# Gate sums of an mLSTM layer: transposes in place of products with the identity, and a running sum by two products over partial sums

## The chip, the cores and the metric

The kernel runs on one core of a Trainium2 chip. The metric is the device time of the whole kernel in microseconds (us), as the median of several runs. The core has five engines that run side by side, each through a queue of its own in the order in which the program was compiled: TensorE (PE in the profile, with its weight loads as PEld), VectorE (DVE), ScalarE (ACT), GpSimd (POOL) and SyncE (SP, which only issues transfers here). Between engines they wait for each other by semaphores.

## The reference, cut to what matters

One decoder layer on 512 positions of 1024 channels. A normed input is projected to the columns of two groups: an mLSTM group of 4 heads of 256 channels, and a convolution group. Both outputs are joined, projected back, normed and added, and a convolutional feed-forward block follows. The change touches the gates of the mLSTM group and one norm of the convolution group. For each head there are two gates per position, an input gate and a forget gate:

```
lfc = jax.nn.log_sigmoid(chunks(f_pre))
...
b = jnp.cumsum(lf_, axis=-1)
dmat = jnp.where(causal, b[..., :, None] - b[..., None, :] + i_[..., None, :], -jnp.inf)
m_t = jnp.maximum(b + m[..., None], jnp.max(dmat, axis=-1))
...
h = num / jnp.maximum(jnp.abs(den), jnp.exp(-m_t))[..., None]
```

The kernel does not carry a state from chunk to chunk. With F the running sum of the log forget gates over all 512 positions and a = i - F, the weight of position s for position t is exp(a[s] - M[t]), where M is the running maximum of a; and exp(-(F + M)) bounds the denominator from below. The convolution group's outcome is normed over its channels, with one factor per position.

## The kernel before, in words

Positions stand as 4 blocks of 128 (NT = 4, P = 128), channels as 8 blocks of 128 (KT = 8). Large products are split into a high and a low part (hi, lo) and done as three products (mm3, L188 to L190). The stages are: reading and norming x; the projections of the convolution group (glu); values and gates of head 0 (make_v, L416); queries, keys and output gates of the heads (head_proj, L481); attention per head (L500); joining (mixa, mixb); the feed-forward block (up); and its last product and the output.

Gates: make_v(0) leaves the eight gate values of each position in gz, 128 partitions by 4 blocks by 8 values. L571 to L581 turn the forget gates into their log sigmoid lf (128 x 4 blocks x 4 heads) with small operations on ScalarE and VectorE. L615 to L618 then make the running sum F over 512 positions by TensorE: the triangle tri gives the sum inside a block, and products with ones, shifted by one, two and three blocks, add the blocks before. VectorE copies it out (Fc, L620) and forms ga = i - F (L621). L624 to L626 turn ga, so that heads stand on 4 partitions and positions along the row (aT). A scan on VectorE makes the running maximum Mr (L628), which is split into Ms (L630, L631) for the weights of each head (make_E, L598). L633 to L636 turn Mr back to positions on partitions (mtok), and L638 to L640 make em of it, the bound of the denominator.

Norm of the convolution group: the helper bcast (L199 to L204) spreads a factor per position over all partitions. It takes a column of 128 factors, lets it stand for 128 columns (to_broadcast), and multiplies it with the identity. It is called once, by rms_bcast (L206) in norm_rows (L772), with the name ry_b.

Order of the work: the queues of SP and TensorE follow the order in which the program is written (manual_schedule, L1333). The order on VectorE, ScalarE and GpSimd is made by a planner, from priorities and from times in its own plan; only the stages inside in_order() (the opening, the stretch between joining and feed-forward, and the output) are fixed by hand. The convolution taps (cv, L731, 25 per block of channels on VectorE, in cv_block at L714) have a lowered priority and fill VectorE's queue between other operations. On TensorE the order about the change is: three projections of head 0 (L611, L612), the running sum (L618), the fourth projection (L622), the turning of ga (L626), the fifth projection (L632), the turning of Mr (L636), the sixth (L642), and then head 0's attention. hn (L549) is the outcome of a head's attention after its norm; it is turned at L555. E (L515) are the products of scores and weights. The identity (ident), ones and tri are float32. A transpose elsewhere in the kernel (L555, L653, L902) is written as PE.transpose with the identity.

Of the kernel before, what the change touches and what calls it, by code (L numbers as in the profile page):

```python
# [10 lines left out]
F32 = mybir.dt.float32  # L11
# [3 lines left out]
ALU = mybir.AluOpType  # L15
PSUM = bass.MemoryType.PSUM

P = 128
# [3 lines left out]
NT = T // P  # L22
H = 4
# [29 lines left out]
def decoder_layer(ctx, tc, w_glu0, x, xT, c, adaT, vecs, w_glu, w_qko, w_v0, w_v, w_out, w_up, w_down, out):  # L53
    nc = tc.nc
    V, S, G, PE = nc.vector, nc.scalar, nc.gpsimd, nc.tensor

    const = ctx.enter_context(tc.tile_pool(name="const", bufs=1))
# [26 lines left out]
    def slot(name, dt=F32):  # L84
        return slots.tile([P, T], dt, tag="t", name=name)

    def mmbank(name):
        return psum.tile([P, T], F32, tag="mm", bufs=4, name=name)

    def atbank(name):  # L90
        return psum.tile([P, T], F32, tag="at", bufs=2, name=name)
# [9 lines left out]
    ident = const.tile([P, P], F32, name="ident")  # L101
    make_identity(nc, ident)
    ones = const.tile([P, P], F32, name="ones")
    V.memset(ones, 1.0)
    tri = const.tile([P, P], F32, name="tri")
# [93 lines left out]
    def bcast(col, n, name, bank=atbank):  # L199

        ps = bank(name)
        for i in range(n // P):
            PE.matmul(ps[:, i * P : (i + 1) * P], col[:, i : i + 1].to_broadcast([P, P]), ident, start=True, stop=True)
        return ps  # L204

    def rms_bcast(ps, n, scale, name, bank=atbank):  # L206
        m = n // P
        t = small.tile([P, NT], F32, tag="rt", name=f"{name}_t")
        V.tensor_scalar(out=t[:, :m], in0=ps[:, :m], scalar1=scale, scalar2=EPS, op0=ALU.mult, op1=ALU.add)
        r = small.tile([P, NT], F32, tag="rr", name=f"{name}_r")  # L210
        G.tensor_tensor(out=r[:, :m], in0=t[:, :m], in1=mhalf[:, :m], op=ALU.pow)
        return bcast(r, n, f"{name}_b", bank)
# [186 lines left out]
    for i in range(G0 // 2, KT):  # L399
        glu_weights(i)  # L400
        for half in range(2):
            ps = mmbank(f"glu{i}_{half}")
# [164 lines left out]
    def g16(name):  # L567
        return const.tile([P, NT, H], F32, name=name)

    fpre = gz[:, :, H : 2 * H]  # L570
    fa, fe, fu, fl, fr, lf = (g16(f"g_{i}") for i in ("fa", "fe", "fu", "fl", "fr", "lf"))  # L571
# [7 lines left out]
    V.tensor_tensor(out=fr, in0=fr, in1=fa, op=ALU.mult)  # L579
    V.tensor_tensor(out=fl, in0=fl, in1=fr, op=ALU.subtract)  # L580
    V.scalar_tensor_tensor(out=lf, in0=fpre, scalar=0.0, in1=fl, op0=ALU.min, op1=ALU.subtract)  # L581
    OFF = [0, 512, 896, 1152]
    NS = [T - cc * P for cc in range(NT)]

# [29 lines left out]

    fps = atbank("fcum")  # L615
    fv = fps[:, : NT * H].rearrange("p (t h) -> p t h", t=NT)
    for d in range(NT):
        PE.matmul(fps[:, d * H : NT * H], ones if d else tri, lf[:, : NT - d, :].rearrange("p t h -> p (t h)"), start=d == 0, stop=d == NT - 1)  # L618
    Fc, ga = g16("Fc"), g16("ga")
    V.tensor_copy(Fc, fv)  # L620
    V.tensor_tensor(out=ga, in0=gz[:, :, :H], in1=Fc, op=ALU.subtract)  # L621
# [1 line left out]

    aps = atbank("aT")  # L624
    for tt in range(NT):
        PE.matmul(aps[:H, tt * P : (tt + 1) * P], ga[:, tt, :], ident, start=True, stop=True)  # L626
    Mr = slot("Mr")[:H, :]
    V.tensor_tensor_scan(out=Mr, data0=aps[:H, :], data1=zero[:H, :].to_broadcast([H, T]), initial=0.0, op0=ALU.max, op1=ALU.max)  # L628

# [3 lines left out]
    mps = atbank("mtok")  # L633
    mv = mps[:, : NT * H].rearrange("p (t h) -> p t h", t=NT)
    for tt in range(NT):
        PE.matmul(mv[:, tt, :], Mr[:, tt * P : (tt + 1) * P], ident[:H, :H], start=True, stop=True)  # L636
    em = g16("em")
    V.tensor_tensor(out=em, in0=Fc, in1=mv, op=ALU.add)  # L638
    S.activation(em, em, AF.Exp, scale=-1.0)
# [394 lines left out]
    for i in range(NF):  # L1034
        if i < NE:
            pa, pg = early[i]
        else:
# [11 lines left out]
            for half in range(2):  # L1049
                ps = mmbank(f"up{i}_{half}")  # L1050
# [141 lines left out]
    for m in range(NM):  # L1192
# [5 lines left out]
        if M2 - NT <= m < M2:  # L1198
            tt = m - M2 + NT
# [138 lines left out]
```

## Time and profile before

| | us |
|---|---|
| median of 3 runs | 772.34 |
| lowest and highest run | 771.94, 775.13 |
| the profiled execution, its span from first to last instruction | 771.4 |
| busy in it: TensorE | 758.4 |
| VectorE | 610.1 |
| ScalarE | 403.8 |
| GpSimd | 352.2 |

The profile is of one execution of its own; the page gives its span, which lies 0.94 us below the median of the timed runs. A page of the profile gives busy times, then the span in forty equal slices with a digit for the busy tenths of each engine, then the chain of work that ended last, followed back from the last instruction to what released each step. Answers of the trace give the same by line, by stage or in order of time. In a timeline a row is a start, a duration and an instruction, several alike merged into one row with their count.

### The profile page before, as it was taken

To read this page: it belongs to the slowest core of one execution; us is meant where nothing else is said; L and a number is where in the kernel's file an instruction comes from. 1 tells how busy PE (TensorE), PEld (TensorE's weight loads), DVE (VectorE), ACT (ScalarE), POOL (GpSimd) and SP (SyncE) were. 2 spreads that over 40 slices of the span, in tenths; PEclk is the share of its full clock that TensorE was granted. 3 is DMA by queue.
4 is the path that set the end of the run, shared out by engine and by line. 5 is a ranking of instruction groups with operands and counts; after the bars stand their busy time and mean duration, and the time that the engine had idled before them with its cause. 6 is when DMAs were issued, how large, how long until landed. Compare 5 with 4: busy or idle time off the path is not lost.

```text
span 771.4 us, 10631 instructions
## 1 busy us (share of the span) xinstructions
PE 758.4 (98%) x3709; PEld 637.5 (83%) x3709; DVE 610.1 (79%) x967; ACT 403.8 (52%) x761; POOL 352.2 (46%) x286
## 2 busy tenths in 40 slices
PE   7999999999999999999999999999999999999996
PEld 5788898778888888988888998888888888888885
DVE  6997999999999966756768798666556687799995
ACT  5447266776666447582253555444444444455762
POOL 2029578696798645443661456444444440000001
PEclk9999999999999999999999999999999999999998
DMA  8983214214022452434953753332233321777872
GB/s 320 377 301 132 90 55 164 82 40 151 30 84 107 153 179 105 164 110 164 366 199 126 253 197 130 130 130 88 110 117 129 130 89 62 255 271 241 298 260 109
DMA packets 36409, 125.33 MB, mean 162 GB/s; under 512 B 4194, under 2 KB 5634, under 8 KB 30468
## 3 DMA queue, kind: packets, MB, share of 16 engines
q1 hardware_dynamic: 24372, 96.17, 35.5%
q10 hardware_dynamic: 11984, 28.48, 10.6%
q8 instruction: 29, 0.48, 0.3%
q14 instruction: 24, 0.20, 0.1%
HBM read 113.22 MB, written 11.42 MB: 162 GB/s over the span
## 4 chain that ended last, share of the span: by engine, by line
PE 72%; DVE 21%; DMA 2%; ACT 2%; issue 2%; POOL 0%; ACTq 0%; DVEq 0%; POOLq 0%
PE up L189 10%; PE up L188 10%; DVE cv L731 10%; PE up L190 10%; PE p L1185 4%; PE glu L189 3%; PE glu L190 3%; PE glu L188 3%; PE p L189 3%; PE p L188 3%; PE p L190 3%; PE mixa L188 2%; PE mixa L190 2%; PE mixa L189 2%; PE mixb L189 2%; PE mixb L188 2%
## 5 line engine op out<-in xcount | busy, mean ns | idle before, releaser
L731 DVE SCALAR_TENSOR_TENSOR cv<-gt,cvw,cv 128x505 f32<-128x505 f32 (+24 forms) x200 | 137.3, 729 | 2.3 <-ACT cv L719 1.1
L685 POOL TENSOR_TENSOR ro2r<-ro2t,mhalf 128x1 f32<-128x1 f32 x1 | 0.5, 537 | 119.8 <-DVE ro2t L683 119.8
L727 POOL TENSOR_TENSOR cs<-cs,cs 128x510 f32<-128x510 f32 (+3 forms) x32 | 41.9, 1308 | 0.3
L171 POOL TENSOR_TENSOR wup_1024l<-wup,wup_1024h 128x512 fp32r<-128x512 f32 x20 | 27.4, 1372 | 31.6 <-ACT wup_1024h L170 31.6
L171 POOL TENSOR_TENSOR wup_0l<-wup,wup_0h 128x512 fp32r<-128x512 f32 x20 | 27.7, 1387 | 30.0 <-ACT wup_0h L170 30.0
L171 POOL TENSOR_TENSOR wup_1536l<-wup,wup_1536h 128x512 fp32r<-128x512 f32 x20 | 28.0, 1399 | 27.6 <-ACT wup_1536h L170 25.1
L155 DVE SCALAR_TENSOR_TENSOR junk<-ada,cb 128x1024 bf16<-128x1024 f32 x20 | 31.3, 1565 | 8.5 <-DMA ada<-in_adaT 8.4
L189 PE MATMUL up<-u2l,wup_0h 128*128 128x512 f32 (+1 forms) x100 | 36.5, 365 | 0.2 <-DVE u2l L910 0.2
L188 PE MATMUL up<-u2h,wup_0h 128*128 128x512 f32 (+1 forms) x100 | 36.5, 365 | 0.0
L188 PE MATMUL up<-u2h,wup_1024h 128*128 128x512 f32 (+1 forms) x100 | 36.4, 364 | 0.0
L190 PE MATMUL up<-u2h,wup_0l 128*128 128x512 f32 (+1 forms) x100 | 36.4, 364 | 0.0
L188 PE MATMUL up<-u2h,wup_512h 128*128 128x512 f32 (+1 forms) x100 | 36.4, 364 | 0.0
L189 PE MATMUL up<-u2l,wup_512h 128*128 128x512 f32 (+1 forms) x100 | 36.4, 364 | 0.0
L190 PE MATMUL up<-u2h,wup_512l 128*128 128x512 f32 (+1 forms) x100 | 36.4, 364 | 0.0
L188 PE MATMUL up<-u2h,wup_1536h 128*128 128x512 f32 (+1 forms) x100 | 36.4, 364 | 0.0
L189 PE MATMUL up<-u2l,wup_1536h 128*128 128x512 f32 (+1 forms) x100 | 36.4, 364 | 0.0
L190 PE MATMUL up<-u2h,wup_1536l 128*128 128x512 f32 (+1 forms) x100 | 36.4, 364 | 0.0
L190 PE MATMUL up<-u2h,wup_1024l 128*128 128x512 f32 (+1 forms) x100 | 36.4, 364 | 0.0
L189 PE MATMUL up<-u2l,wup_1024h 128*128 128x512 f32 (+1 forms) x100 | 36.3, 363 | 0.0
L171 POOL TENSOR_TENSOR wup_512l<-wup,wup_512h 128x512 fp32r<-128x512 f32 x20 | 27.7, 1383 | 14.0 <-ACT wup_512h L170 14.0
L725 ACT ACTIVATE cs<-gt,cvw 128x511 f32<-128x511 f32 (+4 forms) x40 | 27.4, 716 | 6.5 <-POOL cs L727 3.2
L170 ACT ACTIVATE wup_1024h<-wup 128x512 fp32r<-128x512 f32 x22 | 13.9, 631 | 25.1 <-PE up L189 20.4
(1072 smaller groups left out, 2667.0 us busy)
## 6 DMA issues: line engine op xcount, KB each, us to landing
wup<-in_w_up SPq DMA_DIRECT2D x22, 1024.0 KB, 6.5
wqko<-in_w_qko SPq DMA_DIRECT2D x12, 1024.0 KB, 4.8
ada<-in_adaT ACTq DMA_DIRECT2D x20, 512.0 KB, 4.6
ada<-in_adaT SPq DMA_DIRECT2D x16, 512.0 KB, 6.9
wo<-in_w_out SPq DMA_DIRECT2D x8, 1024.0 KB, 4.8
spare<-in_adaT ACTq DMA_DIRECT2D x12, 512.0 KB, 7.4
wd<-in_w_down SPq DMA_DIRECT2D x6, 768.0 KB, 6.7
g2kept<-g2d SPq DMA_DIRECT2D x11, 384.0 KB, 7.3
```

Of the source, the lines that this page charges most:

```text
L155: t = V.scalar_tensor_tensor(out=junk, in0=r, scalar=1.0, in1=cb, op0=ALU.mult, op1=ALU.mult, accum_out=mod[:, i : i + 1])
L170: S.activation(hi[:, :n], src, AF.Copy)
L171: (eng or G).tensor_tensor(out=lo[:, :n], in0=src, in1=hi[:, :n].bitcast(F32), op=ALU.subtract)
L188: PE.matmul(ps, a[0], b[0], start=start, stop=False)
L189: PE.matmul(ps, a[0], b[1], start=False, stop=False)
L190: PE.matmul(ps, a[1], b[0], start=False, stop=stop)
L685: G.tensor_tensor(out=r, in0=t, in1=mhalf[:, :1], op=ALU.pow)
L725: S.activation(t[:, d:], cvx[j][:, : T - d], AF.Copy, scale=w(CK - 1 - d))
L727: G.tensor_tensor(out=side[:, d:], in0=side[:, d:], in1=t[:, d:], op=ALU.add)
L731: last_tap[0] = V.scalar_tensor_tensor(out=cp[:, d:], in0=cvx[j][:, : T - d], scalar=w(CK - 1 - d), in1=cp[:, d:], op0=ALU.mult, op1=ALU.add)
L1185: PE.matmul(ps[q], x, y, start=False, stop=m == NM - 1 and i == 2, skip_group_check=True)
```

## The change: what it does

Five edits. In bcast, at L626 and at L636 the product with the identity becomes a transpose against the identity. The running sum becomes two products in place of four: one of the triangle with all of lf, and one of ones with a new tile, before, that holds for the second, third and fourth block the sum of the blocks ahead of it. That tile is made on VectorE by two additions and a copy of 128 x 4 elements behind lf.

```
@@ bcast
-            PE.matmul(ps[:, i * P : (i + 1) * P], col[:, i : i + 1].to_broadcast([P, P]), ident, start=True, stop=True)
+            PE.transpose(ps[:, i * P : (i + 1) * P], col[:, i : i + 1].to_broadcast([P, P]), ident)
@@ behind lf (L581)
+    before = const.tile([P, NT - 1, H], F32, name="g_before")
+    V.tensor_tensor(out=before[:, 1, :], in0=lf[:, 0, :], in1=lf[:, 1, :], op=ALU.add)
+    V.tensor_copy(before[:, 0, :], lf[:, 0, :])
+    V.tensor_tensor(out=before[:, 2, :], in0=before[:, 1, :], in1=lf[:, 2, :], op=ALU.add)
@@ running sum (L617)
-    for d in range(NT):
-        PE.matmul(fps[:, d * H : NT * H], ones if d else tri, lf[:, : NT - d, :].rearrange("p t h -> p (t h)"), start=d == 0, stop=d == NT - 1)
+    PE.matmul(fps[:, : NT * H], tri, lf.rearrange("p t h -> p (t h)"), start=True, stop=False)
+    PE.matmul(fps[:, H : NT * H], ones, before.rearrange("p t h -> p (t h)"), start=False, stop=True)
@@ gate sums turned (L626)
-        PE.matmul(aps[:H, tt * P : (tt + 1) * P], ga[:, tt, :], ident, start=True, stop=True)
+        PE.transpose(aps[:H, tt * P : (tt + 1) * P], ga[:, tt, :], ident)
@@ maximum turned back (L636)
-        PE.matmul(mv[:, tt, :], Mr[:, tt * P : (tt + 1) * P], ident[:H, :H], start=True, stop=True)
+        PE.transpose(mv[:, tt, :], Mr[:, tt * P : (tt + 1) * P], ident[:H, :H])
```

## The prediction

> **What bounds the kernel now.** I read the page first: busy time, the forty slices and the chain that ended last.
>
> ```profile
> span 771.4 us, 10631 instructions
> ...
> PE 758.4 (98%) x3709; PEld 637.5 (83%) x3709; DVE 610.1 (79%) x967; ACT 403.8 (52%) x761; POOL 352.2 (46%) x286
> ...
> PE   7999999999999999999999999999999999999996
> PEld 5788898778888888988888998888888888888885
> DVE  6997999999999966756768798666556687799995
> ...
> PE 72%; DVE 21%; DMA 2%; ACT 2%; issue 2%; POOL 0%; ACTq 0%; DVEq 0%; POOLq 0%
> ```
>
> TensorE is busy for 758.4 of 771.4 us, so at first sight every microsecond taken from it should come off the end. But 21% of the chain that ended last is VectorE, and the slices show VectorE full from the third to the fourteenth. Next I read what TensorE waited for, the chain in order of time, and the busy time by stage.
>
> ```profile
> PE s L514 <- DVE E L515: 0.4, 1, 0.4
> PE hT L555 <- DVE hn L549: 0.4, 1, 0.4
> PE s L514 <- DVE so L557: 0.3, 1, 0.3
> ```
> ```profile
> 118.40 0.36 DVE g_fu L575
> ...
> 196.42 5.76 DVE cv L731 x9
> 202.18 1.04 DVE hn L549 x4
> ...
> 270.88 0.48 DVE E L515
> 271.40 0.71 PE s L514 x4
> ```
> ```profile
> 131.00:140.00 9.00, 9.00 (x48) 7.08 (x48) 9.00 (x17) 4.66 (x8) 4.97 (x4) 1.00 0.36 118
> ...
> 160.00:180.00 20.00, 20.00 (x91) 16.62 (x91) 20.00 (x33) 12.80 (x26) 17.10 (x15) 1.00 0.34 120
> 180.00:202.00 22.00, 22.00 (x132) 19.67 (x131) 21.94 (x35) 15.67 (x35) 16.28 (x15) 1.00 0.16 59
> ...
> 260.00:300.00 40.00, 39.23 (x174) 31.38 (x173) 26.28 (x38) 21.05 (x47) 22.11 (x15) 1.00 0.48 161
> ...
> 450.00:600.00 150.00, 150.00 (x676) 124.78 (x675) 98.46 (x125) 69.27 (x113) 79.43 (x57) 1.00 0.36 126
> ```
>
> In a row by stage the numbers after the first (the length) are busy time of PE, PEld, DVE, ACT and POOL, then the granted clock. Two engines are full at once from 118 to 202 us: TensorE with products, VectorE with convolution taps (cv, L731) among which the gate arithmetic is threaded. TensorE's only stop there is the 0.4 us before the transposes of hn at 202.58, and there it is VectorE that is late: hn stood behind nine taps. The next stops, 0.77 us in the stretch 260 to 300, are VectorE's again (E and so). So from 118 to 271 us the end is set by VectorE's queue, with TensorE less than half a microsecond ahead; from 271 us until the output stage it is set by TensorE alone (150.00 of 150.00). Three of the four edited places of TensorE lie in the first stretch, one in the second.
>
> **What the change takes from TensorE.** In the timeline of TensorE each row is a start, a duration, and the instructions merged into it. What a block costs is the distance from its start to that of the next work, since consecutive matmuls overlap.
>
> ```profile
> 131.73 0.29 PE L618 MATMUL fcum<-g_lf,tri 128*128 128x16 f32 x2
> 131.87 0.81 PE L618 MATMUL fcum<-g_lf,ones 128*128 128x12 f32 x6
> 132.53 0.49 PE L188 MATMUL qko<-uh,wqko_1024h 128*128 128x512 f32 x1
> ...
> 138.21 1.04 PE L626 MATMUL aT<-ident,ga 128*4 128x128 f32 x8
> 139.18 0.50 PE L188 MATMUL qko<-uh,wqko_0h 128*128 128x512 f32 x1
> ...
> 144.87 1.05 PE L636 MATMUL mtok<-ident,Mr 4*128 4x4 f32 x8
> 145.84 0.50 PE L188 MATMUL qko<-uh,wqko_1024h 128*128 128x512 f32 x1
> ...
> 324.50 1.11 PE L203 MATMUL ry_b<-ident,ry_r 128*128 128x128 f32 x8
> 325.36 0.48 PE L188 MATMUL mixa<-wo_512h,hh 128*128 128x512 f32 x1
> ...
> 409.18 1.03 PE L902 MATMUL xT<-ident,un 128*128 128x128 f32 x8
> 409.97 0.48 PE L188 MATMUL mixb<-wo_0h,yh 128*128 128x512 f32 x1
> ```
>
> Each of the four edited blocks is four calls in the program and eight instructions in the trace: a float32 product runs as two. The transposes of L902 are eight calls (two banks of four) and eight instructions, in 0.79 us. So a transpose is one instruction where the product was two, at the same 0.10 to 0.12 us apiece. The running gate sum goes from four products to two, which is four instructions. Every block should halve: L618 from 0.80 to 0.40, L626 from 0.97 to 0.49, L636 from 0.97 to 0.49, L203 from 0.86 to 0.43. Saved are 0.40 + 0.48 + 0.48 = 1.36 us ahead of 202 us, and 0.43 us at 324 us.
>
> The 0.43 us of L203 lies where TensorE alone sets the end, and TensorE shows no stop there; I count it in full. The 1.36 us lie in VectorE's stretch. The first of it is lost at once: the weights of L626 already wait for ga, which VectorE writes.
>
> ```profile
>   DVE ga L621: 0.4, 1
> ```
>
> A TensorE that comes 0.40 us sooner from L618 waits 0.40 us longer here, and what L626 and L636 save waits at 202.58, for hn. What is late next is VectorE itself. I count 0 of the 1.36 us, and keep 1.36 us as the other bound.
>
> **What it adds to VectorE.** Three instructions on 128x4 elements behind lf: two additions and a copy. The nearest rows are those of the gate arithmetic on 128x16, with GpSimd's beside them.
>
> ```profile
> 125.04 0.65 DVE L580 TENSOR_TENSOR g_fl<-g_fl,g_fr 128x16 f32<-128x16 f32 x1
> ...
> 127.54 0.66 DVE L581 SCALAR_TENSOR_TENSOR g_lf<-gz,g_fl 128x16 f32<-128x16 f32 x1
> ...
> 137.82 0.16 DVE L621 TENSOR_TENSOR ga<-gz,Fc 128x16 f32<-128x16 f32 x1
> 137.91 0.74 DVE L462 SCALAR_TENSOR_TENSOR k_2c<-qko,vec,k_2c 128x510 f32<-128x510 f32 x1
> ```
> ```profile
> 124.37 1.29 POOL L171 TENSOR_TENSOR wqko_1024l<-wqko,wqko_1024h 128x512 fp32r<-128x512 f32 x1
> ...
> 126.87 1.30 POOL L171 TENSOR_TENSOR wqko_0l<-wqko,wqko_0h 128x512 fp32r<-128x512 f32 x1
> 128.13 1.29 POOL L171 TENSOR_TENSOR wqko_512l<-wqko,wqko_512h 128x512 fp32r<-128x512 f32 x1
> 132.10 1.29 POOL L171 TENSOR_TENSOR wqko_1024l<-wqko,wqko_1024h 128x512 fp32r<-128x512 f32 x1 [2.68 <-ACT wqko_1024h L170]
> ```
>
> The same size costs 0.16 us at L621 (the next instruction starts after 0.09) and 0.65 us at L580 and L581. Those two end at 125.69 and 128.20, and GpSimd's instructions end at 125.66 and 128.17: the small operation waited until GpSimd's ended. The Trainium skill has this as a rule (SBUF — State Buffer, "Who interferes with whom"): a VectorE instruction with two SBUF inputs and a GpSimd instruction that reads SBUF exclude each other for the whole instruction. These rows agree with it, and the two new additions are of that kind.
>
> So the bounds for the three are 3 x 0.09 = 0.27 us, if GpSimd is idle, and 0.27 + 3 x 1.29 = 4.1 us, if each meets the start of a GpSimd instruction. Dependent operations of the gate chain start 2.5 us apart (125.04, 127.54), with other work threaded between. By that spacing the first addition and the copy fall near 130.0, where GpSimd is idle (129.4 to 132.1), and the second addition near 132.5, which may meet the instruction of 132.10 and wait up to 0.9 us. I take a third of that, 0.3, so 0.57 us in all. VectorE has hardly any idle time between here and 202 to absorb it, so hn and the work after it come 0.57 us later.
>
> The second product of the gate sum now waits for the second addition. Due near 131.9 us, it may get it at 132.6 to 133.5: a stop of up to 1.6 us. Queued behind it on TensorE is the fourth projection of head 0, and behind that all the rest. This is covered: TensorE has 1.36 us saved and 0.4 us of waiting at 202, together 1.76 us. VectorE does not read the sums before 135.8 us (Fc), and has taps to do.
>
> The sum, against the span: 771.4 + 0.57 - 0.43 = 771.54. The median of the runs is 772.34, 0.94 above the span; with the same distance the forecast is **772.5 us**, no change that can be told.
>
> One page speaks of the transposes otherwise. The Trainium skill (TensorE: Matmul & The Clock Gate, "Part 4: PE-mode transpose") gives about 275 ns for one transpose in a kernel's context.
>
> ```profile
> L902 PE MATMUL xT<-ident,un x32: 270/272/273, 409.2 to 432.9; 128*128 128x128 f32 x32
> ```
>
> The trace agrees with that figure as the duration of one (0.272), but eight of them passed in 0.79 us. Taken as the price of each, the page's figure would make L203 4 x 0.275 = 1.1 us instead of 0.43, and the sum 0.67 us longer, an estimate.
>
> **The rivals.**
>
> *All of TensorE's saving arrives.* VectorE's order is not written out here (only SP's and TensorE's are); the planner puts hn, ga and E where it finds their inputs ready. If TensorE's results come sooner in its plan, hn moves ahead of some of its nine taps. Then 1.79 us come off: 770.55. With the stops at 202 and 271 gone too (0.4 and 0.77), 769.4. For it: the nine taps are filler. Against it: VectorE is full in any case. Chance 0.18.
>
> *Locks or the new wait cost more.* Three additions that each wait a whole GpSimd instruction give + 4.1 - 0.4 = 776.0; an addition threaded one spacing of 2.5 us later makes the stop of TensorE 4.1 instead of 1.6 us, 2.4 over the cover, and gives 772.34 + 2.4 - 0.43 = 774.3. Against it is GpSimd's idle stretch. Chance 0.13.
>
> *The order slips the wrong way* (the rival on the slower side). Three more instructions and other instants of TensorE make the planner thread VectorE anew, and hn, or the E of a later head, lands behind more taps. One tap is 5.76 / 9 = 0.64 us, all of it TensorE's stop at 202.58. From six more taps on it is slower than 0.5%; nine more give 772.5 + 5.8 = 778.3. For it: the order already has one such group ahead of hn. Against it: the plan moves by a microsecond, the size of one or two taps. Chance 0.13.
>
> *The transposes are not cheaper*: each costs its duration on TensorE, 0.27 us. L203 then costs 0.22 us more, the other two with L618 stay within the wait at 202, and with VectorE's 0.57 that is 773.1. The pitch at L902 speaks against it: 0.03.
>
> **How the numbers follow.** The forecast has the remaining 0.53. A measurement of this kernel tells about 0.5%, 3.9 us, from no change: 768.5 to 776.2. The first rival's best case stays above 768.5, so faster gets 0.03, for an order that also helps later stages; slower gets the third rival's 0.13; same the rest, 0.84. The range goes from 769.4, rival one with the stops gone, up to 776.4, just above the second rival's upper end; the third rival and the surprise on the faster side stay outside.
>
> **What would show it.** TensorE 1.8 us less busy apart from new stops; the four blocks at half their length and four instructions; a longer wait at L626 and at L555 for VectorE; the additions at 0.1 to 0.2 us or stretched to the end of a GpSimd instruction; the start of s at 271.4 moved by under 1 us, and the distance from there to the end shorter by 0.43 us. It would be wrong if the waits of TensorE before 271 us vanish (first rival), if L618 stops for over 1.8 us (second), if more than a handful of taps stand ahead of hn or E (third), or if the transposes are spaced by 0.27 us.

## The result, and the profile after

| | before | after |
|---|---|---|
| median, us | 772.93 (6 runs, the three of the table above among them) | 778.03 (6 runs) |
| lowest and highest run | 771.94, 775.13 | 776.60, 779.30 |
| ratio, 95% interval | | 1.0065 (1.0049 to 1.008) |

The kernel became 0.65% slower, 5.1 us, against a forecast of no change. 778.03 lies above the upper end of the range (776.4).

The profiled execution of after took 776.86 us, 1.2 us less than its median. So the two traced spans differ by 3.7 us, the medians by 5.1; what is read from the traces below accounts for the 3.7. The page of after, with the rows that answer to those of before:

```profile
span 775.1 us, 10601 instructions
...
PE 757.8 (98%) x3693; PEld 636.2 (82%) x3693; DVE 616.6 (80%) x970; ACT 406.5 (52%) x763; POOL 352.5 (45%) x286
...
PE 76%; DVE 16%; ACT 4%; issue 2%; DMA 1%; POOL 0%; ACTq 0%; DVEq 0%; POOLq 0%
```

TensorE has 16 instructions fewer, as the change says, but only 0.6 us less busy time. VectorE has three instructions more and 6.5 us more busy time. ScalarE has two instructions more, and nothing in the change gives it any. Those two lead to the cause.

The waits of TensorE in after (us in total, times, longest):

```profile
PE s L514 <- ACT E L613: 2.8, 1, 2.8
...
PE fcum L622 <- DVE g_before L585: 1.4, 1, 1.4
```

The 0.4 us for hn at L555 is gone; those for E and so are 0.6 and 0.5. Two long stops are new: the one that the prediction named, at the running sum, and a longer one before head 0's scores, for which ScalarE is named. A third new one, for hn of the last head, takes 0.4 us. The timeline of TensorE in after shows where they stand:

```profile
131.08 0.29 PE L621 MATMUL fcum<-g_lf,tri 128*128 128x16 f32 x2
132.78 0.39 PE L622 MATMUL fcum<-g_before,ones 128*128 128x12 f32 x2 [1.41 <-DVE g_before L585]
133.03 0.48 PE L188 MATMUL qko<-uh,wqko_1024h 128*128 128x512 f32 x1
...
138.65 0.60 PE L630 MATMUL aT<-ident,ga 128*4 128x128 f32 x4
139.00 0.48 PE L188 MATMUL qko<-uh,wqko_0h 128*128 128x512 f32 x1
...
144.66 0.41 PE L640 MATMUL mtok<-ident,Mr 4*128 4x4 f32 x4
144.99 0.50 PE L188 MATMUL qko<-uh,wqko_1024h 128*128 128x512 f32 x1
...
156.26 1.02 PE L514 MATMUL s<-q_0c,k_2c 128*128 128x512 f32 x2
...
160.92 0.91 PE L514 MATMUL s<-q_0c,k_2c 128*128 128x384 f32 x2 [2.78 <-ACT E L613]
...
163.40 0.63 PE L190 MATMUL qko<-uh,wqko_1024l 128*128 128x512 f32 x1
163.83 0.63 PE L188 MATMUL qko<-uh,wqko_1024h 128*128 128x512 f32 x1
...
166.22 0.40 PE L189 MATMUL qko<-ul,wqko_1024h 128*128 128x512 f32 x1
166.46 0.39 PE L190 MATMUL qko<-uh,wqko_1024l 128*128 128x512 f32 x1
...
169.43 0.59 PE L514 MATMUL s<-q_0c,k_2c 128*128 128x256 f32 x2
```

The same three blocks of scores in before:

```profile
157.14 1.02 PE L514 MATMUL s<-q_0c,k_2c 128*128 128x512 f32 x2
...
158.85 0.81 PE L514 MATMUL s<-q_0c,k_2c 128*128 128x384 f32 x2
...
165.60 0.59 PE L514 MATMUL s<-q_0c,k_2c 128*128 128x256 f32 x2
```

Put side by side, TensorE's starts say where the time went. The opening ran 0.65 us sooner in this execution, which is put down to chance and not to the change: e4 and e10 below, which have before's order up to there, start the running sum at 130.62 and 132.56.

| TensorE starts, us | before | after | difference |
|---|---|---|---|
| running sum | 131.73 | 131.08 | -0.65 |
| head 0, first scores | 157.14 | 156.26 | -0.88 |
| second scores | 158.85 | 160.92 | +2.07 |
| third scores | 165.60 | 169.43 | +3.83 |
| end of the span | 771.4 | 775.1 | +3.7 |

Up to the first scores the change has won 0.23 us: the stop of 1.41 at the running sum has eaten most of what the halved blocks gave. Then 2.95 us are lost at the second scores and 1.76 more before the third, 4.7 in all. After that the difference falls to 2.8 us at head 1's first scores and is back at 3.7 at the end. So nearly the whole loss of this execution lies between 157 and 170 us.

The second part of it is no wait. From 163.40 the projection's products start 0.43 us apart; from 166.22 on, and in before, 0.23. The row by stage for this stretch (the granted clock is the number behind GpSimd's count, 0.91; before had 1.00) gives 20 x 0.09 = 1.8 us, which is the 1.76:

```profile
160.00:180.00 20.00, 19.08 (x77) 15.34 (x78) 16.94 (x28) 16.81 (x34) 17.95 (x15) 0.91 0.22 80
```

The stop itself is read from ScalarE's timeline. In before:

```profile
149.07 0.62 ACT L463 ACTIVATE k_3c<-k_3c 128x512 f32<-128x512 f32 x1
149.71 1.28 ACT L639 ACT_TABLE_LOAD   x1
151.00 0.22 ACT L639 ACTIVATE em<-em 128x16 f32<-128x16 f32 x1
...
154.38 0.39 ACT L607 ACTIVATE E<-Md,ga 128x128 f32<-128x128 f32 x1
```

And in after:

```profile
148.71 0.60 ACT L741 ACTIVATE gt<-cv 128x512 f32<-128x512 f32 x1 [3.00 <-DVE cv L735]
...
150.14 1.28 ACT L643 ACT_TABLE_LOAD   x1
151.44 0.22 ACT L643 ACTIVATE em<-em 128x16 f32<-128x16 f32 x1
...
152.20 1.28 ACT L463 ACT_TABLE_LOAD   x1
153.49 0.63 ACT L463 ACTIVATE k_3c<-k_3c 128x512 f32<-128x512 f32 x1
...
157.50 1.28 ACT L611 ACT_TABLE_LOAD   x1
158.79 0.40 ACT L611 ACTIVATE E<-Md,ga 128x128 f32<-128x128 f32 x1
```

ScalarE loads a table when it goes from Silu to Exp or back. In before the last key block of head 0 (k_3c, Silu, L463) came ahead of em (Exp), so em and the weights E shared one load. In after the planner put em first: Exp, Silu, Exp, and thus two loads of 1.28 us more (the two new instructions of ScalarE). E begins at 158.79 instead of 154.38, 4.4 us later. The two loads are 2.6 of it. Most of the rest is that the Silu and one more activation (cs, L729) now stand between em and E, 1.2 us, and a start 0.4 us later, behind an idle stretch of 3.00 us in which ScalarE waited for a tap of VectorE. L613 in after (L609 in before) is the part of E that reads the tile Mb, which lies in one of the two banks that the scores use in turn. So TensorE's second block of scores waited for the last of L613, 2.78 us.

Of VectorE's 6.5 us, some 2.8 are seen in three rows of its timeline in after, with one row of GpSimd's behind them:

```profile
131.47 1.26 DVE L585 TENSOR_TENSOR g_before<-g_before,g_lf 128x4 f32<-128x4 f32 x1
...
137.87 0.73 DVE L625 TENSOR_TENSOR ga<-gz,Fc 128x16 f32<-128x16 f32 x1
...
145.49 1.77 DVE L635 TENSOR_TENSOR Ms<-Mr,Ms 4x512 fp32r<-4x512 f32 x1
```
```profile
131.45 1.26 POOL L171 TENSOR_TENSOR wqko_1024l<-wqko,wqko_1024h 128x512 fp32r<-128x512 f32 x1 [2.68 <-PE fcum L621]
```

The second addition began 0.02 us after a GpSimd instruction and ended 0.02 us after it: 1.26 us for 128 x 4 elements. ga took 0.73 and Ms 1.77, where they had taken 0.16 and 0.68 in before: the same operations, which now lie beside GpSimd instructions that start at 137.27 and 145.43. Another 2.2 us are the scalings of head 0's hn, of which the experiments tell.

### The profile page after: what moved, and what is told of

The parts are those of the page before. It is cut to its first block, busy times and chain, and to the rows that moved or that the text cites. A ratio compares the mean times of both kernels' runs of the same rounds, so it can differ in the third digit from the quotient of the medians.

```text
span 775.1 us, 10601 instructions
## 1 busy us (share of the span) xinstructions
PE 757.8 (98%) x3693; PEld 636.2 (82%) x3693; DVE 616.6 (80%) x970; ACT 406.5 (52%) x763; POOL 352.5 (45%) x286
## 4 chain that ended last, share of the span: by engine, by line
PE 76%; DVE 16%; ACT 4%; issue 2%; DMA 1%; POOL 0%; ACTq 0%; DVEq 0%; POOLq 0%
PE up L189 10%; PE up L188 10%; PE up L190 10%; DVE cv L735 7%; PE p L1189 4%; PE glu L190 3%; PE glu L188 3%; PE glu L189 3%; PE p L189 3%; PE p L188 3%; PE p L190 3%; PE glu L316 2%; PE mixa L188 2%; PE mixa L190 2%; PE mixa L189 2%; PE mixb L190 2%
## 5 line engine op out<-in xcount | busy, mean ns | idle before, releaser
L735 DVE SCALAR_TENSOR_TENSOR cv<-gt,cvw,cv 128x502 f32<-128x502 f32 (+24 forms) x200 | 137.5, 729 | 2.4 <-ACT cv L723 1.1
L729 ACT ACTIVATE cs<-gt,cvw 128x511 f32<-128x511 f32 (+4 forms) x40 | 27.3, 716 | 4.7 <-POOL cs L731 3.7
```

The source lines that it names most:

```text
L729: S.activation(t[:, d:], cvx[j][:, : T - d], AF.Copy, scale=w(CK - 1 - d))
L735: last_tap[0] = V.scalar_tensor_tensor(out=cp[:, d:], in0=cvx[j][:, : T - d], scalar=w(CK - 1 - d), in1=cp[:, d:], op0=ALU.mult, op1=ALU.add)
```

## The experiments

Two theories stood at the start. **Theory 1**: the new order on ScalarE (two table loads) makes the stop at head 0's scores, and the clock behind the stop makes it dearer. **The rival** (theory 2 in the expectations): the running sum costs it, by VectorE's three operations and the stop at L622. Each run below was timed against the kernel before on the same chip; that kernel's median was 772.55 for the first four, 771.65 for the next four and 771.80 for the last four.

**e1: the three transposes alone**, the running sum as before (the diff is against after).

```
-    before = const.tile(...)   # and its two additions and copy
-    PE.matmul(fps[:, : NT * H], tri, ...); PE.matmul(fps[:, H : NT * H], ones, before ...)
+    for d in range(NT): PE.matmul(fps[:, d * H : NT * H], ones if d else tri, ...)
```

> The three transposes alone, with the running sum of before (four products, no new tile). In the compiled order of ScalarE the exponential of em stands ahead of the Silu of head 0's last key block, as in the changed kernel, with 14 table loads in place of 12. Theory 1 (the loss is this order: two more table loads make head 0's weights E late, TensorE stops for them and then runs at a lower clock): a stop of 2 to 3 us ahead of head 0's second score block, a granted clock under 1 behind it, and 775 to 778 us. Theory 2 (the loss is the new wait at the running sum and the operations locked out by GpSimd, carried on by VectorE's queue): neither is here, so 771 to 773 us.

Measured: 775.15 (774.94 to 775.84), ratio 1.0038 (1.0026 to 1.0049). ScalarE has em ahead of k_3c, with 14 table loads as in after, so the transposes alone turn the order round. But the stop of the scores behind it was only 1.0 us, and two others were longer:

```profile
PE s L514 <- DVE so L557: 2.0, 1, 2.0
PE hT L555 <- ACT E L609: 1.4, 1, 1.4
...
PE s L514 <- ACT E L609: 1.0, 1, 1.0
```

The granted clock behind that stop stayed at 1.00; it was 0.91 from 202 to 220 us, behind the stop of 2.0. The time agrees with theory 1, the place only in part.

**e2: the running sum alone**, the products with the identity as before (against after).

```
-            PE.transpose(...)                       # bcast, aT, mtok
+            PE.matmul(..., ident, start=True, stop=True)
```

> The running sum by two products with the new tile, alone; the other three places as before. ScalarE's order has em behind the Silu of the last key block and 12 table loads, as before. Theory 1: a stop of about 1.4 us at the running sum, no long stop at head 0's scores, the clock at 1.0, and 772 to 774 us. Theory 2: the same loss as the changed kernel, 776 to 778 us.

Measured: 777.97 (776.9 to 779.26), ratio 1.0073 (1.006 to 1.0086), though ScalarE keeps before's order and its 12 table loads. This contradicts theory 1 as the whole story: the sum alone loses as much as the whole change, and it does it elsewhere. Its waits of TensorE, and the stretch from 202 us by stage:

```profile
PE s L514 <- DVE so L557: 2.6, 1, 2.6
...
PE fcum L622 <- DVE g_before L585: 1.4, 1, 1.4
```
```profile
202.00:220.00 18.00, 14.44 (x68) 10.69 (x67) 17.93 (x29) 12.26 (x26) 10.93 (x10) 0.91 0.09 30
```

Here TensorE waits for so, which VectorE multiplies behind hn, and again the clock is 0.91 behind the stop. VectorE's timeline in e2, and GpSimd's below it, show why VectorE was late:

```profile
194.37 5.24 DVE L549 TENSOR_SCALAR hn<-hn,fac 128x256 f32<-128x256 f32 x4
...
201.42 7.75 DVE L735 SCALAR_TENSOR_TENSOR cv<-gt,cvw,cv 128x489 f32<-128x489 f32 x12
209.08 1.27 DVE L557 SCALAR_TENSOR_TENSOR so<-so,hT 128x512 f32<-128x512 f32 x2
```
```profile
194.26 1.29 POOL L754 TENSOR_TENSOR ysum<-ysum,gt 128x512 f32<-128x512 f32 x1
195.52 1.34 POOL L171 TENSOR_TENSOR wqko_0l<-wqko,wqko_0h 128x512 fp32r<-128x512 f32 x1
196.82 1.33 POOL L731 TENSOR_TENSOR cs<-cs,cs 128x509 f32<-128x509 f32 x1
198.11 1.34 POOL L753 TENSOR_TENSOR ysq<-ysq,ydl 128x512 f32<-128x512 f32 x1
```

The four scalings of hn took 1.13 us together in before's timeline (the prediction quotes the 1.04 of them that lie on the chain that ended last), and 5.24 here: one GpSimd instruction each. In before they began at 202.09, when GpSimd was idle (200.75 to 205.39); in e2 the planner put them some eight microseconds sooner, beside a full queue. Hence a **third theory, the lock**: wherever the new order puts hn beside a busy GpSimd, VectorE loses 2 to 4 us, and what stands behind it comes late. That a tensor_scalar can exclude GpSimd is stated by the Trainium skill too (SBUF — State Buffer, "Who interferes with whom"), which counts it among the operations that can enter a two-port mode; these rows agree. In e1 the four took 5.24 us as well, in after 3.33.

**e3: after, with em held behind k_3c's Silu on ScalarE.** This undoes the changed order there; on VectorE and on GpSimd one pair of neighbours each changes places besides, and all other instructions of the two keep the order of after.

```
-        S.activation(t, t, AF.Silu)                  # conv4
+        last_silu[0] = S.activation(t, t, AF.Silu)
-    S.activation(em, em, AF.Exp, scale=-1.0)
+    e = S.activation(em, em, AF.Exp, scale=-1.0)
+    tc.add_manual_dep(e.ins, last_silu[0].ins.name, ...)   # an order, no semaphore
```

> The changed kernel, with one more dependency: the exponential of em may not stand ahead of the Silu of head 0's last key block on ScalarE. The new wait and the operations on VectorE stay. Theory 1: no long stop at head 0's scores, the clock at 1.0 there, the stop at the running sum still 1.4 us, and 771 to 773.5 us. Theory 2: the pin changes nothing, 776 to 778 us.

Measured: 773.53 (772.61 to 775.42), ratio 1.0015 (1.0002 to 1.0027). ScalarE has 12 table loads again, the wait for E L613 is gone, and the granted clock from 160 to 180 us is 1.00. After lay 5.1 us above the kernel before that was timed with it, e3 lies 1.0 above its own: 4.1 us are given back, where theory 1 had 2.8 + 1.8 = 4.6 for stop and clock. So the order on ScalarE is what most of the loss of the changed kernel needs. That it needs nothing else doesn't follow; e9 comes back to this. What is left is this:

```profile
PE s L515 <- DVE so L558: 1.7, 2, 1.2
PE fcum L623 <- DVE g_before L586: 1.5, 1, 1.5
```

**e4: the transposes of the norm factors alone** (bcast as in after, all else as before).

```
-            PE.matmul(ps[...], col[...].to_broadcast([P, P]), ident, start=True, stop=True)
+            PE.transpose(ps[...], col[...].to_broadcast([P, P]), ident)
```

> The transposes of the norm factors alone; the order on ScalarE and GpSimd is that of before, on VectorE one pair of neighbours changes places. Both theories: the block at 0.43 us or less in place of 0.86, four instructions in place of eight, no new stop, and 772.5 us, 0.4 less than before. If transposes made TensorE's clock fall, it would be under 1 behind this block and the kernel slower.

Measured: 771.19 (770.68 to 772.3), ratio 0.9985 (0.9977 to 0.9994). The block took 0.37 us instead of 0.86. By the interval the gain is 0.5 to 1.8 us, which holds the 0.49 saved: it arrives in full where TensorE alone sets the end. The median is 0.9 us lower still. The stop for so at head 2, 0.33 us in before, is absent in this trace; the rest is left open.

**e5: after, with idle time of TensorE filled.** Head 0's first block of scores is done three times over, which leaves its values as they are, so that TensorE has four products of 512 columns more, 1.7 us, where it stood still. The question was whether the clock falls for the stop's sake.

```
+            if h == 0 and cc == 0:
+                for d in 2 * list(range(2)):
+                    PE.matmul(sp[:, :n], ks[d][:, ...], qs[d][:, ...], start=d == 0, stop=d == 1)
```

> The changed kernel, with head 0's first score block done three times over into the same bank (the repeats change no value): 1.72 us of TensorE work that nobody needs, put where TensorE stood still for 2.78 us. Theory clock (TensorE's clock falls behind a stop of over some 2 us): the stop falls to about 1.1 us, the products behind it come 0.23 us apart and not 0.43, the granted clock of the stretch 160 to 180 is 1.00 and not 0.91, and the third score block starts 1.8 us sooner, though TensorE has more to do; 776 us. Rival (the lower clock comes with the transposes or with the sort of work there): it stays at 0.91, and the time at 778 us or more.

Measured: 780.01 (778.14 to 781.17), ratio 1.0106 (1.0086 to 1.0125), a miss against the 776 expected. The row for 160 to 180 us has a clock of 1.00, and the products behind the scores start 0.23 us apart, as expected. But the planner threaded VectorE anew from 160 us on, and other stops came: 2.7 us for E in three pieces, 1.7 us for hn. The clock's part is supported in that place; of the sum nothing follows.

**e6: the running sum alone, hn scaled on ScalarE** (e2 with the scalings of hn moved off the engine that GpSimd locks out).

```
-            V.tensor_scalar(out=hv, in0=hv, scalar1=fac[:, tt : tt + 1], scalar2=None, op0=ALU.mult)
+            S.activation(hv, hv, AF.Copy, scale=fac[:, tt : tt + 1])
```

> The running sum by two products alone (the second experiment), with the four scalings of hn by their factors on ScalarE instead of VectorE, for each head. Theory lock (the second experiment lost its time because the four scalings of hn waited for a GpSimd instruction each, 5.24 us in place of 1.13, so that Md, E and so of head 1 came late behind them): no stop of TensorE over 1 us between 195 and 215 us, the clock at 1.0 there, and 771 to 774 us, with the stop of 1.4 us at the running sum still there. Theory 2 (the stop at the running sum and VectorE's three operations carry to the end): 777 to 778 us, as before.

Measured: 771.64 (771.16 to 773.69), ratio 1.0001 (0.9992 to 1.001): the loss of e2, 5.4 us, is gone. The same twelve taps stand ahead of so as in e2 (7.74 us), and so starts at 204.58 instead of 209.08. The edit takes the scalings off VectorE whole, the 1.13 us that they cost without a lock included; a run in which only the lock is missing was not made. Of the new stops only the one at the running sum is left, 1.5 us.

**e7 and e8: the transposes alone with em held (e7), and with hn on ScalarE besides (e8).** Edits as in e1 and e3, and as in e6.

> The three transposes alone, with the exponential of em held behind the Silu of head 0's last key block. Theory 1 with the order on ScalarE alone: 771 to 772 us, the stops of 1.0, 1.4 and 2.0 us gone. Theory lock: only the stop of 1.0 at head 0 goes; if the scalings of hn still meet GpSimd at work (5.24 us for four), the stops at head 1 stay and it is 773 to 775 us.

> As the one before, with the scalings of hn on ScalarE. Theory lock: no stop of TensorE over 1 us at head 0 or 1, clock 1.0 throughout, and 769.5 to 771.5 us, less than before by the 1.3 us of the three blocks and more. If theory 1 is all there is, the same time as the one before.

Measured: e7 771.95 (771.63 to 774.05), ratio 1.0001 (0.9992 to 1.001), 0.3 us above its own before where e1 was 2.6 above, so 2.3 us are given back, as theory 1 had it. Apart from ScalarE's order only one pair of neighbours on VectorE differs from e1. Its hn still took 5.24 us, but the stop behind it was 1.5 us and the clock stayed at 1.00, so the lock was cheaper here than the third theory had it. e8 768.45 (768.31 to 768.82), ratio 0.9955 (0.9943 to 0.9968): behind the opening TensorE stops for 0.2 us only. With both cures the transposes bring 3.2 us: 0.62 + 0.64 + 0.49 from the three blocks, and before's stops of 0.4 and 0.77 make 2.9 of it.

**e9: after, with hn on ScalarE only** (em not held).

> The changed kernel whole, with the scalings of hn on ScalarE and nothing else; em's exponential still stands ahead of the Silu of the last key block, with two table loads more. If the order on ScalarE is what the changed kernel loses by, the stop of 2.8 us at head 0's second score block and the lower clock behind it stay, and it is 775 to 778 us. If it is the locks on hn alone, 771 to 773 us.

Measured: 773.71 (771.28 to 775.57), ratio 1.0021 (1.0012 to 1.003), between the two expectations and with a wide spread. The profiled execution was its fastest, 771.28, and shows the clock in a new place, behind the stop at the running sum. The stretch 131 to 140 us by stage, in e9 and then in after:

```profile
131.00:140.00 9.00, 7.69 (x29) 6.06 (x30) 9.00 (x16) 2.56 (x5) 3.78 (x3) 0.81 0.30 117
```
```profile
131.00:140.00 9.00, 7.59 (x38) 6.00 (x37) 9.00 (x15) 4.01 (x7) 4.48 (x4) 1.00 0.30 117
```

A stop of 1.49 us in e9 and of 1.41 in after; the clock fell in the one and not in the other, and 9 x 0.19 = 1.7 us are lost. The stop for E at head 0's second scores is absent in this execution, though ScalarE still has em ahead of k_3c and 14 table loads. These rows of e9 show why:

```profile
157.07 0.40 ACT L611 ACTIVATE E<-Md,ga 128x128 f32<-128x128 f32 x1
...
159.19 0.91 PE L514 MATMUL s<-q_0c,k_2c 128*128 128x384 f32 x2
```

Counted from the running sum (130.53 in e9, 131.08 in after), the slow clock brought TensorE to head 0's first scores 1.7 us later than in after (157.39 against 156.26). E came 1.2 us sooner, since ga and Ms met less of GpSimd's work (0.17 and 1.09 us in place of 0.73 and 1.77). Together that is a little more than the 2.78 us of the stop. Up to 194 us e9 and after have the same order on VectorE, ScalarE and GpSimd, so this differs by execution and not by the edit. Whether the slower executions of e9, up to 775.57, have the stop isn't shown, as only the fastest was traced. So the order on ScalarE costs its stop only if E is late enough for TensorE, and by the medians moving hn alone gives back 3.2 of the 5.1 us: the two cures overlap and don't add up.

**e10: before, with hn on ScalarE**, the control for that edit.

> The kernel before, with the scalings of hn on ScalarE: none of the change. The scalings take 1.13, 2.17, 2.17 and 1.14 us there, so little is to be had: the stops of 0.4 us at hn and 0.77 us at head 2 go, 770 to 771.5 us. If the eighth experiment's gain came from this edit alone, 768.5 us.

Measured: 771.94 (771.5 to 773.58), ratio 1.0002 (0.9993 to 1.0011). By itself the edit brings nothing; what it saves in e6 and e8 is a loss that the new orders make.

**e11 and e12: after, with the second addition early.** Both hold em behind k_3c and put the second addition ahead of the first tap of the second query block; e11 has hn on ScalarE besides.

```
-    V.tensor_tensor(out=before[:, 2, :], ...)
+    before2[0] = V.tensor_tensor(out=before[:, 2, :], ...)
...
+            if name == 'q0_1' and d == 1:
+                behind(tap, before2[0])
```

> The changed kernel whole, with em's exponential held behind the last key's Silu, the scalings of hn on ScalarE, and the second addition of the new tile ahead of the first tap of head 0's second query block on VectorE. By the locks, the addition then starts before GpSimd's next instruction and takes 0.1 us, so that TensorE does not stop at the running sum. No stop over 1 us, clock 1.0, 767.5 to 769 us: the eighth experiment less up to 0.4 us for the shorter running sum.

> The changed kernel with em's exponential held back (the third experiment) and the second addition ahead of that tap; hn on VectorE. Theory 2 (the stop at the running sum carries to the end): 1.4 us less than the third experiment's 773.5. Theory lock: the stop at the running sum is gone, but TensorE waits as much longer for so and E at head 1, 772.5 to 774 us.

Measured: e11 768.22 (767.77 to 769.09), ratio 0.9952 (0.994 to 0.9964), the best version and better than both kernels. e12 770.54 (769.86 to 773.81), ratio 0.9984 (0.9974 to 0.9993). In e11 the additions take 0.15 us each, none meets GpSimd, and the longest wait of TensorE behind the opening is this one:

```profile
PE aT L634 <- DVE ga L629: 0.5, 1, 0.5
```

e12 against e3 differs only in the early addition, and in order only by a few neighbours between 129 and 138 us: 0.9984 against 1.0015, about 2.4 us, where the stop taken away was 1.5. The stop at the running sum was not free there. The traces show 1.9 us of the 2.4: TensorE's stops from 118 to 300 us sum to 3.7 us in e3 and 1.7 in e12. The stop of 1.45 went and one of 0.47 for ga came, and those for so fell from 1.7 to 0.4.

## Why the prediction was wrong, point by point

**The blocks of TensorE: right.** Four instructions each. Turning ga passed in 0.35 us (forecast 0.49), the maximum in 0.33 (0.49), the norm factors in 0.37 (0.43); the running sum took 0.36 for both products where no wait parts them (e11; forecast 0.40). The transposes pass at less than 0.1 us apiece, far from the 0.27 of the last rival. Where nothing takes it back this arrives: e4, e8, e11.

**The additions: right in kind, mis-sized.** The first and the copy fell at 129.4 and 129.5, where GpSimd was idle, as placed. The second met GpSimd, and the next instruction started 1.18 us after it (131.47 to 132.65) instead of 0.09: 1.1 us more, where I had a bound of 0.9 and took a third of it. The stop at L622 came with 1.41 us, within "up to 1.6".

**"This is covered": not shown, and partly wrong.** With em and hn put right in different ways the answer differs. e6, with a stop of 1.5 us, is no slower than e10 without one; but e12, without it, is 2.4 us faster than e3, with it. Most of that lies in stops, the one at the running sum and those for so behind it; whether the clock fell behind the first in the executions of e3 that were not traced, as it did in e9's, isn't shown.

**The step that failed** is "From 118 to 271 us the end is set by VectorE's queue ... I count 0", with "What is late next is VectorE itself". I followed one queue that the planner makes, VectorE's, and never read the other one, ScalarE's, for what stands next to what. The margin there was in sight: k_3c's Silu, a table load and em's Exp stood in a row from 149.07. In after the planner changed the order on VectorE too: em's operand comes at 149.22, ahead of k_3c's last tap at 149.29, where before had the tap at 146.88 and em at 148.20:

```profile
149.22 0.17 DVE L642 TENSOR_TENSOR em<-Fc,mtok 128x16 f32<-128x16 f32 x1
149.29 0.74 DVE L462 SCALAR_TENSOR_TENSOR k_3c<-qko,vec,k_3c 128x509 f32<-128x509 f32 x1
```

On ScalarE em stands first likewise. e1 shows that the transposes suffice for both and e2 that the sum does not. Why the planner chose so isn't shown: its own times are in no trace. e3 shows that holding the order on ScalarE alone gives back 4.1 of the 5.1 us. The third rival was of this kind, at a chance of 0.13; I put the slip on taps ahead of hn, at 0.64 us apiece, and argued that "the plan moves by a microsecond, the size of one or two taps". That argument is what failed: where two instructions change places, the price is not the shift of the plan but what stands between them, here two table loads of 1.28 us and the bank that E holds.

**Two prices were missing from every case.** A stop of TensorE was priced at its length, but behind the stop of 2.78 us the clock cost another 1.8 us, and behind that of e2 as much (18 x 0.09 = 1.6). And the lock was weighed for the three new operations alone, though the same rows (L580, L581) said that a small VectorE operation with two SBUF inputs that moves may meet a GpSimd instruction, as ga and Ms did. The scalings of hn wait too, with 1.13 us before and 3.33 to 5.24 in several of the new orders; no row ahead of the prediction showed that.

**VectorE as what bounds 118 to 202 us** is not refuted. e10 shows no gain from taking the scalings off it, and e7 no gain from TensorE's savings, while together (e8) they give 3.2 us. That the two engines run level there, so that either one alone gains nothing, fits this; it isn't shown, since e7's order also made hn 4.1 us longer. One reading of the slices was off and nothing hangs on it: VectorE's fourth slice is a 7, and it is full from the fifth to the fourteenth.

## What to carry to other kernels

Where a planner makes the order, an edit of under two microseconds may be decided, as here, by the neighbours that it makes change places: look on every queue, ScalarE's too, for pairs whose inputs come within a microsecond of each other, and price the exchange (a table load each way, a whole GpSimd instruction for each small VectorE operation) before counting what the edit saves. If the trace after shows a count of ScalarE's instructions that the edit doesn't explain, compare the table loads first. An order that was found and is good can be held with one dependency. Here that alone gave back the loss but no gain (e3); the saving arrived in full once hn was moved off VectorE and the second addition was placed early as well (e11).

## What the runs showed of the hardware

The granted clock fell to about half for some 3.4 us (0.43 us from product to product instead of 0.23) behind stops of TensorE of 1.49 us (e9), 1.99 (e1), 2.63 (e2) and 2.78 (after). It did not fall behind 1.41 (after and e2), 1.5 (e3, e6 and e7) or 1.7 (e5, a stop for hn). Length alone doesn't decide it: 1.49 with and 1.7 without. The Trainium skill (TensorE: Matmul & The Clock Gate, Part 1) tells of a free-running window of some 3.4 us, and of a clock that falls after a whole idle one. The slow stretches are about as long as such a window; that idle time has to last a whole one doesn't agree with these rows, in which stops of 1.5 to 2.8 us were enough. What else decides, the runs leave open.

Four scalings of 128 x 256 elements cost VectorE 1.13 us beside an idle GpSimd (before) and 5.24 us beside a busy one (e2). On ScalarE the same four took 1.7 us, and the time shows nothing of it (e10).
